# Two rotary chunks of an input projection moved ahead of the gates' chunks, in a two-layer diffusion trunk on one core

## The chip, the core and the metric

The kernel runs on one NeuronCore of a Trainium2 chip. The metric is the time of one launch on the device, in microseconds. The core has five engines with instruction queues of their own, and each works through its queue in order: PE (TensorE, matrix products), DVE (VectorE), ACT (ScalarE), POOL (GpSimd), and SP (SyncE), which issues nearly all DMAs here. A weight load of PE is shown apart, as PEld.

## The reference, cut to what matters

Two layers over 9 blocks of 128 tokens: block 0 is the prompt, blocks 1 to 8 are latent tokens on a grid. Each layer projects its input `h` once, splits the result, and feeds three mixers:

```
z = einsum('bsd,dn->bsn', h, w_in[l])
hq, hff, hfb, hi, hg, mq, mkv, mkr, gq, gk, gv = split(z, IN_OFFSETS)
hg_out = _hgrn_mixer(hq, hff, hfb, hi, hg, ...)      # gated scan, forward and backward
q_nope, q_pe = _mla_queries(mq, ...); ckv = _rms(mkv, ...)
gq = _rope_2d(_rms(gq, gqa_q_norm), row, col)        # latent tokens only
gk = _rope_2d(_rms(gk, gqa_k_norm), row, col)
mixed = concat([hg_out, mla_out, gqa_out]); y = mixed @ w_out[l]
```

The scan needs the query part `hq`, the two gates `hff`, `hfb` and the input `hi`. The rotary queries and keys `gq`, `gk` are wanted by the second attention alone. A layer norm, a SwiGLU and another layer norm end the layer. All of it is float32; most products are made of three passes on a high and a low half of the operands.

## The kernel before, in words

A layer is phase_b (input projection and forward scan), phase_c (both attentions, with the backward scan beside them), phase_d (output projection) and phase_e (SwiGLU). The change is in `phase_b`.

The projection's columns are cut into chunks of 256 (the last of 288). Chunk 0 is `hq`, written transposed. The others go through `token_chunk`: the weights are loaded and split into halves (`w_in`, `wsplit`), and for each of the 9 token blocks 24 products of 128x256 (three passes, eight slices of the depth) fill one PSUM buffer, which an evacuation function then takes away. I call one such block of a chunk a *tile*. Chunks 1 and 2 are the gates (`ev_f`: two sigmoids on ACT), 4 and 3 are `hi` and `hg` (`ev_raw`: a copy and a store), 5 and 6 are the rotary queries and keys (`ev_q`), `"b"` holds the keys and values (`ev_k`), and 7 the queries of the other attention (`ev_m`).

`ev_q` is the long one. ACT squares the tile and copies it to a stage buffer (L403, L404); DVE sums the squares (L407); POOL makes the reciprocal root in two instructions (L118, L119); DVE scales by it and by the norm's weights (L410, L412, the latter twice in chunk 6); POOL turns the pairs in `rope` (two products L392, one L395, one sum L396; not for block 0); SP stores the result to DRAM (L419). There are three stage buffers for all evacuations (`stage`, tag `st`), and a buffer is free again when its store has landed. PSUM buffers for the tiles: two in layer 0, three in layer 1 (`banks`, ring `A`).

`gates` takes logarithms, and `hgrn` is the scan: for each of the 9 token blocks a `prep` (transposes and running sums), eight levels (`levels`: DVE makes differences L636 and L639, ACT exponentials L641, POOL two products L643 and L645, PE small products L650, DVE a masked copy L655), and `out` (L674, L677, L684). I call these nine *scan blocks*. The stores of all chunks (`zq`, `zi` and so on) are read back from DRAM by later steps.

`gqa_turn` reads the stored rotary queries and keys back (L521, L525, L526), transposes them on PE (L529), and splits them on ACT and POOL (L532, L536, L537, L104); ten such turns for head group 1 are written in the loop of chunk 7, but their buffers lie where the scan's buffers (`b`) lay, so they can't start before the scan has ended. The attention's first transposed probabilities (L801) follow.

What sets the order on the engines: the instructions are handed to a scheduler that lists them per engine by a model of the time, the earlier written ones first, later written ones where an engine would wait. So chunks written behind `hgrn` are woven into its gaps on PE. In layer 0 `self.fill()` adds, at four tiles of each chunk, a step of the modulation's products (L177) from a generator.

Of the kernel before, what the change touches and what calls it, by code (L numbers as in the profile page):

```python
# [53 lines left out]
class Build:  # L54
# [275 lines left out]
    def phase_b(self, l, first=None):  # L330
# [19 lines left out]
        def token_chunk(name, evac):  # L350
            ws = self.w_in(*name)
            n = 288 if name[1] == "b" else 256
            for t in range(NT):
                ps = self.ps("A")
                terms = [(self.hts(t, k, 0), self.hts(t, k, 1), hi[:, k - k0, :], lo[:, k - k0, :])
                         for k0, k1, hi, lo in ws for k in range(k0, k1)]
                self.mm3(ps[:, :n], terms)
                evac(t, ps)
                if t % 2:
                    self.fill()  # L360

        def stage():
            return self.t("b2", [P, 384], tag="st", bufs=3)

        def ev_raw(name):
            def ev(t, ps):
                st = stage()
                nc.scalar.copy(st[:, :256], ps[:, :256])
                nc.sync.dma_start(z[name][t], st[:, :256])
            return ev  # L370

        def ev_f(d):
            def ev(t, ps):
                nc.scalar.activation(lf[:, d, t, :], ps[:, :256], AF.Sigmoid)
                self.last_sig = nc.scalar.activation(kk[:, d, t, :], ps[:, :256], AF.Sigmoid, scale=-1.0)  # L375
            return ev

        def tables(t):
            tb = self.t("b2", [P, 192], tag="tb", bufs=2)
            nc.sync.dma_start(tb, A["rope_tok"][:, t - 1, :])  # L380
            return tb

        def rope(x, tb, off, heads, half):

            w = 4 * half
            xv = x.rearrange("p (h a s f) -> p h a s f", h=heads, a=2, s=2)
            cos = tb[:, off:off + w].unsqueeze(1).broadcast_to([P, heads, w])
            sin = tb[:, off + w:off + 2 * w].rearrange("p (a s f) -> p a s f", a=2, s=2)
            t2 = self.tmp()
            tv = t2[:, :heads * w].rearrange("p (h a s f) -> p h a s f", h=heads, a=2, s=2)  # L390
            for s in range(2):
                nc.gpsimd.tensor_tensor(tv[:, :, :, s, :], xv[:, :, :, 1 - s, :],  # L392
                                        sin[:, :, s, :].unsqueeze(1).broadcast_to([P, heads, 2, half]), op=ALU.mult)
            xm = x.rearrange("p (h w) -> p h w", h=heads)
            nc.gpsimd.tensor_tensor(xm, xm, cos, op=ALU.mult)  # L395
            nc.gpsimd.tensor_tensor(x, x, t2[:, :heads * w], op=ALU.add)  # L396

        def ev_q(half):
            def ev(t, ps):
                st = stage()  # L400
                x = st[:, :256]
                sq = self.tmp()
                nc.scalar.activation(sq[:, :256], ps[:, :256], AF.Square)  # L403
                nc.scalar.copy(x, ps[:, :256])  # L404
                ss = self.t("small", [P, 4], tag="ss4", bufs=3)
                r = self.t("small", [P, 4], tag="r4", bufs=3)
                nc.vector.reduce_sum(ss, sq[:, :256].rearrange("p (h f) -> p h f", h=4), axis=AX.X)  # L407
                self.rsq(r, ss, 1 / 64, 4)
                xv = x.rearrange("p (h f) -> p h f", h=4)
                nc.vector.tensor_tensor(xv, xv, r.unsqueeze(2).broadcast_to([P, 4, 64]), op=ALU.mult)  # L410
                for h0, n, g in (((0, 4, 0),) if half == 0 else ((0, 2, 0), (2, 2, 64))):
                    nc.vector.tensor_tensor(xv[:, h0:h0 + n], xv[:, h0:h0 + n],  # L412
                                            rows[:, g:g + 64].unsqueeze(1).broadcast_to([P, n, 64]), op=ALU.mult)
                if t == 0:
                    if half:
                        nc.sync.dma_start(A["o_gk"][0, l].rearrange("s h f -> s (h f)"), x[:, 128:256])
                else:
                    rope(x, tables(t), 0, 4, 16)
                nc.sync.dma_start(z["q"][t][:, half * 256:half * 256 + 256], x)  # L419
            return ev  # L420
# [30 lines left out]
        for ci in range(3):  # L451
            for j in range(2):
# [3 lines left out]
                         for k0, k1, hi, lo in ws for k in range(k0, k1)]  # L456
# [4 lines left out]
                nc.sync.dma_start(z["h"][3 * ci:3 * ci + 3, :, j, :].rearrange("t p s -> p t s"),  # L461
                                  sg[:, :384].rearrange("p (t s) -> p t s", t=3))

        token_chunk((l, 1), ev_f(0))
        cst = {}
        for name, n in (("uinc", 2), ("ustr", 1)):
# [16 lines left out]
        self.hgrn(l, cst, masks)  # L483

        token_chunk((l, 3), ev_raw("g"))
        token_chunk((l, 5), ev_q(0))
        token_chunk((l, 6), ev_q(1))

        self.close("b")
        self.open("gB", side="right")  # L490
# [933 lines left out]
```

## Time and profile before

| | us |
|---|---|
| median of 3 runs | 3805.0 |
| the runs | 3798.03 to 3807.32 |
| the profiled execution | 3800.49 |
| its span, first to last instruction | 3798.7 |
| PE busy | 3690.6 (97%) |
| DVE, ACT, POOL busy | 2009.7, 1384.2, 1100.6 |

The profile shows one execution. Its page gives busy times and the granted clock of PE; the trace behind it gives each instruction's start and length. In a row of busy time by stretch, "x" counts instructions, and PEclk is the mean of the granted clock, 1.00 for 2.4 GHz and 0.50 for 1.2 GHz. A PE that waits inside a run of small products can still be shown as busy, so busy time is an upper bound of work.

### The profile page before, as it was taken

The page shows a single profiled execution, that of the slowest core. Times are in us where ns is not written, and L with a number is a line of the kernel's source. Part 1 is how long each engine was busy: PE and PEld are TensorE (multiplying, and loading weights), DVE is VectorE, ACT ScalarE, POOL GpSimd, SP SyncE. Part 2 cuts the span into 40 slices and gives each one's busy share as a digit, 9 for nine tenths or more (in the row PEclk, how much of TensorE's full clock was granted, in tenths as well). Part 3 has the DMA queues.
Part 4 walks back from the last instruction along what each step waited for, and adds up shares of the span by engine and source line. Part 5 has one row for each costly group of instructions (what it writes and reads, how often), then busy time and mean ns, then how long its engine had stood idle before and what let it go on. Part 6 is the DMA issues. An engine that isn't in the chain of part 4 may idle for free.

```text
span 3798.7 us, 60408 instructions
## 1 busy us (share of the span) xinstructions
PE 3690.6 (97%) x23734; PEld 3206.4 (84%) x23734; DVE 2009.7 (53%) x3906; ACT 1384.2 (36%) x3285; POOL 1100.6 (29%) x1394
## 2 busy tenths in 40 slices
PE   8999999999999999999999988999999999999997
PEld 6887877788788888888989878778887999999996
DVE  3488466556654333333366893665557533333336
ACT  3433476665331111111144334666654211111111
POOL 1168751111260000000432786511126600000054
PEclk9998999999999999999999998999999999999998
DMA  6321520001242122212331114100012311111121
GB/s 231 114 75 62 172 58 19 15 7 34 65 155 81 61 78 73 78 67 78 102 124 57 53 44 132 35 19 15 7 54 65 122 35 50 45 39 45 45 95 72
DMA packets 185967, 263.78 MB, mean 69 GB/s; under 512 B 68657, under 2 KB 114353, under 8 KB 185170
## 3 DMA queue, kind: packets, MB, share of 16 engines
q1 hardware_dynamic: 185682, 259.92, 21.6%
q8 instruction: 187, 3.06, 0.3%
q14 instruction: 98, 0.80, 0.1%
HBM read 218.47 MB, written 38.77 MB: 68 GB/s over the span
## 4 chain that ended last, share of the span: by engine, by line
PE 83%; DVE 6%; POOL 3%; ACT 3%; issue 2%; DMA 2%; SPq 0%; DVEq 0%; POOLq 0%; ACTq 0%
PE b L110 10%; PE b L112 10%; PE b L111 10%; PE d L850 7%; PE c L801 5%; PE a L110 5%; PE a L112 5%; PE a L111 5%; PE b L779 4%; PE a L779 3%; PE b L650 2%; PE c L110 2%; PE c L112 2%; PE c L111 2%; PE d L177 2%
## 5 line engine op out<-in xcount | busy, mean ns | idle before, releaser
L110 PE MATMUL b<-h,w 128*128 128x384 f32 x1848 | 625.4, 339 | 0.1
L111 PE MATMUL b<-h,w 128*128 128x384 f32 x1848 | 622.6, 337 | 2.1 <-DVE h L104 1.3
L112 PE MATMUL b<-h,w 128*128 128x384 f32 x1848 | 622.1, 337 | 0.0
L103 ACT CAST w<-raw 128x1024 fp32r<-128x1024 f32 (+2 forms) x192 | 198.5, 1036 | 808.1 <-PE b L111 153.9
L104 DVE TENSOR_TENSOR w<-raw,w 128x1024 fp32r<-128x1024 f32 (+3 forms) x188 | 239.9, 1281 | 455.4 <-ACT w L103 287.8
L1240 POOL TENSOR_TENSOR acc<-acc,lg 128x512 f32<-128x512 f32 x36 | 50.9, 1432 | 1285.2 <-DVE acc L1226 1281.1
L110 PEld LDWEIGHTS b<-h,w 128*128 128x128 f32 x1848 | 347.6, 188 | 26.4 <-issue 8.4
L111 PEld LDWEIGHTS b<-h,w 128*128 128x128 f32 x1848 | 348.0, 188 | 11.3 <-issue 4.2
L112 PEld LDWEIGHTS b<-h,w 128*128 128x128 f32 x1848 | 347.8, 188 | 7.0 <-issue 4.2
L850 PE MATMUL d<-pt,v 128*64 128x128 f32 x3456 | 288.8, 285 | 0.4 <-DVE m L851 0.4
L110 PE MATMUL a<-w,h 128*128 128x256 f32 (+1 forms) x960 | 284.8, 297 | 0.0
L111 PE MATMUL a<-w,h 128*128 128x256 f32 (+1 forms) x960 | 279.7, 291 | 0.0
L112 PE MATMUL a<-w,h 128*128 128x256 f32 (+1 forms) x960 | 278.8, 291 | 0.0
L801 PE MATMUL c<-ident,p 128*128 128x128 f32 x1728 | 271.4, 279 | 6.2 <-ACT p L785 2.4
L850 PEld LDWEIGHTS d<-pt,v 128*64 128x64 f32 x3456 | 186.4, 136 | 76.4 <-issue 61.2
L780 DVE TENSOR_REDUCE m<-b 128x1 f32<-128x384 f32 x346 | 188.2, 553 | 106.7 <-PE b L779 106.2
L801 PEld LDWEIGHTS c<-ident,p 128*128 128x128 f32 x1728 | 200.0, 141 | 46.6 <-issue 16.8
L785 ACT ACTIVATE p<-b,nm 128x384 f32<-128x384 f32 x346 | 198.5, 582 | 73.3 <-DVE nm L783 67.1
L110 PEld LDWEIGHTS a<-w,h 128*128 128x128 f32 x960 | 185.6, 193 | 24.7 <-ACT m L375 9.2
L111 PEld LDWEIGHTS a<-w,h 128*128 128x128 f32 x960 | 185.6, 193 | 6.0 <-issue 1.9
L112 PEld LDWEIGHTS a<-w,h 128*128 128x128 f32 x960 | 185.5, 193 | 5.3 <-issue 1.7
L103 ACT CAST m<-gate 128x384 fp32r<-128x384 f32 x132 | 67.7, 513 | 324.6 <-DVE gate L1197 324.6
(391 smaller groups left out, 8492.1 us busy)
## 6 DMA issues: line engine op xcount, KB each, us to landing
w<-in_w_ada_dram SPq DMA_DIRECT2D x96, 512.0 KB
raw<-in_w_ffn_in_dram SPq DMA_DIRECT2D x88, 512.0 KB
raw<-in_w_ffn_out_dram SPq DMA_DIRECT2D x44, 512.0 KB
raw<-in_w_in_a_dram SPq DMA_DIRECT2D x32, 512.0 KB
xs<-acc SPq DMA_DIRECT2D x36, 256.0 KB
u<-xs SPq DMA_DIRECT2D x36, 256.0 KB
raw<-in_w_out_dram SPq DMA_DIRECT2D x16, 512.0 KB
tx<-zq SPq DMA_DIRECT2D x72, 96.0 KB
```

The source lines that it names most:

```text
L103: self.nc.scalar.copy(hi, src)
L104: (eng or self.nc.vector).tensor_tensor(lo, src, hi.bitcast(F32), op=ALU.subtract)
L110: self.nc.tensor.matmul(out, ah, bh, start=i == 0, stop=False)
L111: self.nc.tensor.matmul(out, ah, bl, start=False, stop=False)
L112: self.nc.tensor.matmul(out, al, bh, start=False, stop=i == n - 1)
L177: self.nc.tensor.matmul(acc[r:r + 32, :], self.cs[:, 2 * (k + a):2 * (k + a) + 32], w[:, a], start=k < 4, stop=k >= 4)
L650: nc.tensor.matmul(ps[:, j * P:(j + 1) * P], X[r, j, :], Q[r, j, :], start=True, stop=True)
L779: nc.tensor.matmul(ps, a, bfn(c * 384, 384), start=k == 0, stop=k == len(ops) - 1)
L780: nc.vector.reduce_max(mx[:, c:c + 1], ps, axis=AX.X)
L785: nc.scalar.activation(pt[:, c * 384:(c + 1) * 384], tiles[c], AF.Exp, bias=nm, accum_out=sm[:, u, c:c + 1])
L801: nc.tensor.transpose(pt[:, (2 * i + u) * P:(2 * i + u + 1) * P], g["p"][u][:, kt * P:(kt + 1) * P], self.ident)
L850: nc.tensor.matmul(po[h * 64:(h + 1) * 64, :P], g["v"](k, h), turned[s // 2][:, o:o + P], start=k == 0, stop=k == 8)
```

## The change

The two calls for chunks 5 and 6 are written ahead of chunk 1, and so come second and third, behind chunk 0; before, they stood behind chunk 3 (seventh and eighth with the scan counted).

```diff
                 nc.sync.dma_start(z["h"][3 * ci:3 * ci + 3, :, j, :].rearrange("t p s -> p t s"),
                                   sg[:, :384].rearrange("p (t s) -> p t s", t=3))
 
+        token_chunk((l, 5), ev_q(0))
+        token_chunk((l, 6), ev_q(1))
         token_chunk((l, 1), ev_f(0))
         cst = {}
@@
         self.hgrn(l, cst, masks)
 
         token_chunk((l, 3), ev_raw("g"))
-        token_chunk((l, 5), ev_q(0))
-        token_chunk((l, 6), ev_q(1))
```

No instruction of the computation is added or removed. What moves is shown at two places of layer 0.

POOL, from the last half-splits of `h` on. Before, the next work of POOL is the scan's (L645, L607):

```order
L104 TENSOR_TENSOR h_72_246<-u_367,h_72_246 128x384
L104 TENSOR_TENSOR h_72_246<-u_383,h_72_246 128x384
L645 TENSOR_TENSOR Q_1637<-qT_1618,E_1632 128x256
L645 TENSOR_TENSOR Q_1654<-qT_1618,E_1649 128x256
L607 TENSOR_TENSOR m_467<-m_467,u_1606 128x2x256
```

After, `rsv`, `r` are the reciprocal root of one tile, `st` its stage buffer, `tb` the table of the rotation:

```order
L104 TENSOR_TENSOR h_72_246<-u_383,h_72_246 128x384
L118 TENSOR_SCALAR rsv_160_693<-ss_158_690 128x4
L119 TENSOR_TENSOR r_159_691<-rsv_160_693,mhalf_76 128x4
L118 TENSOR_SCALAR rsv_166_731<-ss_164_728 128x4
L119 TENSOR_TENSOR r_165_729<-rsv_166_731,mhalf_76 128x4
L392 TENSOR_TENSOR t_738<-st_724,tb_736 128x8x16 x2
L395 TENSOR_TENSOR st_724<-st_724,tb_736 128x256
L118 TENSOR_SCALAR rsv_176_781<-ss_174_778 128x4
L396 TENSOR_TENSOR st_724<-st_724,t_738 128x256
L119 TENSOR_TENSOR r_175_779<-rsv_176_781,mhalf_76 128x4
L392 TENSOR_TENSOR t_788<-st_774,tb_786 128x8x16 x2
```

All 18 tiles of the two chunks follow one another here, in this pattern, and the rotation of a tile (L392) stands directly behind the root of the same tile (L119).

PE, around the end of the scan. Before, the last `out` (`c_3288`) lies among tiles of chunk `"b"` (`a_4740`, `a_4787`) and modulation steps (`d_4602`), and twelve tiles follow it:

```order
L112 MATMUL a_4740<-w_4505,h_72_246 128x288
L177 MATMUL d_4602<-w_4783,csr_86 32x512 x2
L177 MATMUL d_4602<-w_4873,csr_86 32x512 x2
L677 MATMUL c_3288<-it_3054,at_3058 128x64
L110 MATMUL a_4787<-w_4493,h_74_250 128x288
L111 MATMUL a_4787<-w_4494,h_74_250 128x288
L112 MATMUL a_4787<-w_4493,h_74_250 128x288
L677 MATMUL c_3288<-it_3054,at_3058 128x64
L674 MATMUL c_3288<-Sf_1576,m_466 128x128
L677 MATMUL c_3288<-it_3054,at_3058 128x64 x2
L110 MATMUL a_4787<-w_4493,h_74_250 128x288
```

After, the last `out` (`c_4172`) has no tile behind it:

```order
L650 MATMUL b_4141<-Q_4138,X_4132 128x128 x2
L650 MATMUL b_4145<-Q_4138,X_4132 128x128 x2
L650 MATMUL b_4158<-Q_4155,X_4149 128x128 x2
L650 MATMUL b_4162<-Q_4155,X_4149 128x128 x2
L677 MATMUL c_4172<-it_3938,at_3942 128x64 x2
L674 MATMUL c_4172<-Sf_2460,m_466 128x128
L677 MATMUL c_4172<-it_3938,at_3942 128x64 x2
L529 MATMUL c_4970<-ident_75,tx_4967 128x128
L529 MATMUL c_4980<-ident_75,tx_4976 128x128 x4
L529 MATMUL c_5030<-ident_75,tx_5026 128x128 x4
```

The twelve tiles now stand inside the scan, and the scan's last levels and the turns (L529) follow one another alone.

## Rows read from the trace of the kernel before

**Rows 1.** The page: span, and busy time of PE over the span
```profile
span 3798.7 us, 60408 instructions
...
PE 3690.6 (97%) x23734; PEld 3206.4 (84%) x23734; DVE 2009.7 (53%) x3906; ACT 1384.2 (36%) x3285; POOL 1100.6 (29%) x1394
```
**Rows 2.** Busy by stretch; layers 0, 1: chunks, scan, tail; us, PE, PEld, DVE, ACT, POOL, PEclk
```profile
72.00:175.00 103.00, 102.34 (x770) 86.94 (x770) 32.57 (x60) 39.10 (x84) 3.92 (x4) 1.00 0.39 130
175.00:425.00 250.00, 242.24 (x1716) 202.19 (x1717) 203.41 (x487) 97.88 (x216) 189.68 (x267) 0.95 0.25 77
425.00:480.00 55.00, 49.10 (x354) 42.61 (x353) 16.48 (x31) 26.51 (x73) 36.89 (x69) 0.97 0.74 206
...
1984.00:2070.00 86.00, 84.93 (x723) 84.12 (x721) 49.93 (x60) 39.50 (x85) 14.63 (x6) 1.00 0.25 78
2070.00:2315.00 245.00, 228.18 (x1636) 201.41 (x1637) 200.00 (x481) 95.52 (x217) 190.54 (x275) 0.92 0.16 49
2315.00:2362.00 47.00, 38.87 (x299) 37.48 (x298) 13.31 (x25) 25.04 (x71) 34.52 (x63) 0.90 0.75 206
```
**Rows 3.** Lines L375, L677, L801 by source: min/median/max ns, first and last start
```profile
L375 ACT ACTIVATE m<-a x18: 377/378/380, 74.5 to 137.0; 128x256 f32<-128x256 f32 x18
L375 ACT ACTIVATE m<-a x12: 380/380/381, 1984.7 to 2029.5; 128x256 f32<-128x256 f32 x12
L677 PE MATMUL c<-it,at x72: 217/275/473, 199.6 to 424.6; 128*128 128x64 f32 x72
L677 PE MATMUL c<-it,at x72: 217/275/477, 2093.9 to 2314.6; 128*128 128x64 f32 x72
L801 PE MATMUL c<-ident,p x864: 270/272/332, 480.1 to 938.6; 128*128 128x128 f32 x173
L801 PE MATMUL c<-ident,p x804: 270/272/476, 2361.8 to 2798.0; 128*128 128x128 f32 x161
```
**Rows 4.** Busy by stretch: single scan blocks, two of each layer
```profile
202.60:229.50 26.90, 26.90 (x193) 21.80 (x193) 16.36 (x45) 10.54 (x22) 12.04 (x15) 1.00 0.28 87
...
336.90:367.90 31.00, 31.00 (x188) 24.77 (x187) 24.92 (x60) 12.22 (x26) 23.98 (x34) 0.75 0.14 41
...
2121.40:2147.10 25.70, 25.70 (x201) 22.79 (x201) 22.30 (x55) 9.78 (x25) 23.24 (x33) 1.00 0.10 30
...
2229.00:2259.10 30.10, 25.82 (x165) 22.98 (x165) 24.97 (x59) 11.38 (x24) 23.76 (x30) 0.82 0.20 63
```
**Rows 5.** The rotary tiles' lines on POOL and DVE by source, 236 to 386 us
```profile
L119 POOL TENSOR_TENSOR r<-rsv,mhalf x17: 1005/1058/1820, 240.7 to 381.5; 128x4 f32<-128x4 f32 x17
L118 POOL TENSOR_SCALAR rsv<-ss x17: 193/253/922, 240.0 to 381.2; 128x4 f32<-128x4 f32 x17
L392 POOL TENSOR_TENSOR t<-st,tb x28: 451/500/638, 249.5 to 374.2; 128x128 f32<-128x128 f32 x28
L395 POOL TENSOR_TENSOR st<-st,tb x14: 723/760/989, 250.4 to 374.8; 128x256 f32<-128x256 f32 x14
L396 POOL TENSOR_TENSOR st<-st,t x14: 721/845/1544, 252.5 to 377.2; 128x256 f32<-128x256 f32 x14
L410 DVE TENSOR_TENSOR st<-st,r x17: 406/754/978, 241.9 to 383.4; 128x256 f32<-128x256 f32 x17
L412 DVE TENSOR_TENSOR st<-st,rows x25: 277/505/846, 243.1 to 385.2; 128x128 f32<-128x128 f32 x16, 128x256 f32<-128x256 f32 x9
```
**Rows 6.** The chain of waits, one piece: a store of 128 KB to DRAM; start, us, what
```profile
412.15 1.74 DMA zs<-it
```
**Rows 7.** The turns: ACT's copies by source; POOL's splits by line, busy us, mean ns
```profile
L532 ACT COPY te<-c x20: 266/588/673, 432.5 to 509.5; 128x512 f32<-128x512 f32 x18, 128x128 f32<-128x128 f32 x2
L532 ACT COPY te<-c x20: 266/586/680, 2322.4 to 2393.5; 128x512 f32<-128x512 f32 x18, 128x128 f32<-128x128 f32 x2
...
L537 POOL TENSOR_TENSOR Q<-te,Q 64x384 fp32r<-64x384 f32 x18 | 18.7, 1040 | 13.2 <-ACT Q L536 12.6
L104 POOL TENSOR_TENSOR K<-te,K 128x128 fp32r<-128x128 f32 x20 | 9.2, 463 | 1.2
```

## The prediction

> **What bounds the kernel now.** I read the page's busy times first, then busy time by stretch for the two input projections, then the lines that open and close their parts, then the instructions that move. PE is busy for 97% of the span [rows 1], so the time can fall only by what PE waits or runs at 1.2 GHz, and it rises by each wait that the change adds. The change touches the stretch from the chunks to the first attention product (L801) of each layer; behind it the order of PE is the same as before. So I ask how much later or earlier the first L801 comes; before, it starts at 480.1 and 2361.8 us [rows 3].
>
> That stretch has three parts [rows 2]. In the chunks (72 to 175, 1984 to 2070) PE is full, DVE has a third to a half of the time, POOL almost nothing (3.9 and 14.6 us). In the scan (225 us in layer 0 and 220.7 in layer 1 from the first to the last `out` product, eight periods of 28.1 and 27.6 us, [rows 3]) PE, DVE and POOL are all at 76 to 97%, with a mean granted clock of 0.95 and 0.92. In the tail PE idles 5.9 of 55 us and 8.1 of 47. All that could be won: idle 7.8 + 5.9 + 16.8 + 8.1 = 39 us, and the stretches at 1.2 GHz, half of whose length is 14 and 24 us: 77 us, 2% of the span.
>
> **What moves, part by part.** Per layer 18 tiles of PE work go to the front with their evacuation; nothing is added or taken away.
>
> *The front.* A tile costs PE 2.8 us: 16 steps between the 1st and 17th tile of layer 1's gates take 44.8 us [rows 3]. In layer 0 seventeen steps take 62.5 us [rows 3], with 17 modulation products between them, so such a product costs 0.9 us. Before the scan, PE has 18 tiles more in each layer, in layer 0 also 16 modulation products (the generator is drawn on earlier), in layer 1 half a `hi` tile less: 50.4 + 14.4 = 64.8 us and 50.4 - 1.4 = 49 us.
>
> But the tiles' evacuation may be slower than PE. In the new order of POOL the rotation of a tile follows directly on its own root, and between the two DVE must scale the tile, while POOL, in order, waits. POOL's own time per tile, by the smallest values [rows 5], is 0.193 + 1.005 + 2 x 0.451 + 0.723 + 0.721 = 3.54 us; the wait for DVE 0.406 + about 0.5 and some 0.1 for two hand-overs (my estimate), so a cycle of 4.5 us. By the medians it is 3.92 + 1.4 = 5.3. The rows were taken beside a scan that keeps DVE and POOL above 75%; at the front DVE is at a third, so I take the smallest. With three stage buffers, ACT can take the 18th tile away only when the 15th has been stored: 13 rotated tiles x 4.5 + 2 unrotated x 1.2 + 4 for the first tile through PE, ACT and DVE + 1.7 for the store [rows 6] = 67 us from the start, and then the copy. PE has PSUM buffers for one more tile in layer 0 and two in layer 1; without waiting it would come to that point after 19 x 2.8 + 14.4 = 68 and 20 x 2.8 = 56 us. So layer 0 loses little (I take 2 us, since the modulation products come bunched), layer 1 about 11 (67 - 56). By the medians the evacuation needs 77 us, and the losses are 10 and 21.
>
> On this the Trainium skill bears, page "Perfetto Trace Analysis", section "Optimizing Scalar/DVE Operations": GpSimd and VectorE share an SBUF read port. By this rule the minima hold where DVE is quiet, and the sum stays 3823; with the medians it would be 3841. No run here shows yet which.
>
> *The scan.* Its blocks now have chunks 3, `"b"` and 7 as filler, 25 tiles instead of 31, and these press less on DVE and POOL (`ev_k` and `ev_m` have one norm and at most 32 columns to turn). Blocks 1 to 6 get some 20 tiles, about as many as before; block 7 gets 1.0 and none in layers 0 and 1, block 8 none in either. What a block costs PE apart from filler is read from one without a rotary tile: 202.6 to 229.5, with 3.4 tiles and 4 modulation products, takes 26.9 us with PE full: 26.9 - 9.5 - 3.6 = 13.8. In layer 1 a block with 3.6 tiles gives 25.7 - 10.1 = 15.6 [rows 4], with rotary work on DVE and POOL beside it; relieved of that I take 15. A tile of 288 columns is counted by its width, 3.15 us. Layer 0, blocks 1 to 6: 6 x 13.8 + 11.2 x 2.8 + 8.9 x 3.15 + 20 products x 0.9 = 160 us. Layer 1: 6 x 15 + 11 x 2.8 + 8.9 x 3.15 = 149 us.
>
> The uncovered blocks the trace doesn't show. From below they are bounded by DVE's own work in a block without rotary tiles, 16.4 us [rows 4]; from above by the slowest blocks with filler, 31.0 and 30.1 [rows 4], where PE stood at 0.75 and 0.82 of its clock. Their 3.1 tiles and 6 products and their 2.8 tiles taken off, these two leave 17 and 22 us. So I take 20 us for block 7, and 17.5 for block 8, which prepares no successor. The scan from first to last `out`: 160 + 37.5 = 198 us (225 before) and 149 + 37.5 = 187 (220.7 before).
>
> Here a rule of the Trainium skill speaks against the change: "Perfetto Trace Analysis", section "Optimization Strategy", says that where regimes are bound by different engines, interleaving them may help. The change takes interleaved work apart. By it alone, with no relief in blocks 1 to 6 (they keep 28.1 and 27.6 us), the scan would be 9 and 17 us longer, and the time 3849. The rows show why I don't follow it that far: all three engines are nearly full in the blocks that it would keep.
>
> *The tail.* Before, twelve tiles of `"b"` and 7 stand between the scan's end and L801 in layer 0 and 13.6 in layer 1's last block and tail, and the ten turns of head group 1 hide below them. Now the turns stand alone, since their buffers come free only with the scan's end. The first copy of a turn came 7.9 and 7.8 us behind the last `out` [rows 3, 7]; nine further turns cost POOL 1.04 + 0.46 = 1.5 us each [rows 7] and cannot go faster; I take 1.8 with the loads, and 2.5 us for scores, maximum and exponentials: 7.8 + 16 + 2.5 = 26 us. Bounds: 22 (1.5 each, 1 us behind them) and 32. What is queued behind these waits on PE is the whole attention. Before it was 480.1 - 424.6 = 55.5 and 2361.8 - 2314.6 = 47.2 us.
>
> **The sum.** Layer 0: 64.8 + 2 (front) - 27 (scan) - 29.5 (tail) = +10.3. Layer 1: 49 + 11 - 33.7 - 21.2 = +5.1. Together some +16 us; I add 2 for a slow start of the attention, whose first products now follow 26 us of little work (in layer 1 before, the tail's clock was already 0.90, [rows 2]). 3800.5 + 18 = 3818.5 for the profiled execution, which is 4.5 below the median of the three runs; on the median 3823.
>
> **The rivals.**
> *Faster.* The relief goes deeper: freed of rotary work, a covered block costs PE 10 us besides its tiles instead of 13.8 and 15. Twelve blocks x 4 to 5 us = 54, and the time is 3823 - 54 = 3769. It turns to a gain where the cost falls by over 1.5 us (18 over 12 blocks). For it: clock and idle time are worst in the blocks with DVE and POOL above 77%. Against it: the block from 202.6 had DVE at 61% and POOL at 45% and cost 13.8 all the same.
> *Even.* Turns at 22 us, no stall in layer 0 and 7 in layer 1, layer 1's blocks at 13.8: 18 - 8 - 6 - 7 = -3, so 3802. For it: each alone is an end of a bound that a row supports.
> *Worse.* Medians at the front (+18) and uncovered blocks that fall to 1.2 GHz as the worst ones did (four, 4 us each, +16): 3857.
> *The change does nothing.* Excluded: the orders differ as shown, on both engines.
>
> **How the numbers follow.** Forecast, slower by 5 to 30 us: 0.47. Even: 0.25. Worse: 0.15. Faster: 0.13, of which half is below 3794. The range must leave out two tenths: from 3794 (-11, the even case in, half of the faster one out) to 3858 (the worse case mostly in). About 0.3% (11 us) is what a measurement of this kernel can tell from no change. Faster by more: 0.13; within: 0.29, the even case and the forecast's lower edge; slower by more: 0.58.
>
> **What would show it.** Right: POOL at 75% or more in the first 70 us of layer 1's chunks and PE waiting there on an evacuation; the last `out` around 465 and 2341 us; some 26 us from it to L801, with PE below half; blocks 2 to 6 free of 1.2 GHz. Wrong: PE full at the front (then POOL's cycle is below 3 us), blocks without tiles above 25 us, turns that start before the scan's end, or covered blocks below 22 us, which would be the gain.

## The result, and the profile of the changed kernel

The changed kernel takes 3868.6 us (median of four, 3867.63 to 3869.89) against 3802.3 for the kernel before on the same chip: ratio 1.0172, interval 1.0159 to 1.0185. It is slower by 66 us. The forecast was slower by 18, at most 3858: the direction held, the size did not.

The page of the changed kernel, span and busy times (before: [rows 1]):

```profile
span 3865.8 us, 60513 instructions
...
PE 3710.2 (96%) x23734; PEld 3221.8 (83%) x23734; DVE 1985.4 (51%) x3906; ACT 1392.6 (36%) x3291; POOL 1088.0 (28%) x1394
```

The span is 67.1 us longer, PE's busy time 19.6. So 47.5 us are new idle time of PE. The rest is shown as busy with the same 23734 instructions: work at 1.2 GHz, or waiting inside a run of products. Where the idle time lies is read from the busy time by stretch, which answers to [rows 2]. First the 18 rotary tiles, then gates and `hi`, then the scan, then the bare turns, for layer 0 and for layer 1 (columns: us, then busy us of PE, PEld, DVE, ACT, POOL, the mean granted clock, DMA share, GB/s):

```profile
74.00:156.00 82.00, 64.14 (x469) 56.08 (x468) 25.96 (x62) 14.89 (x38) 51.91 (x90) 0.94 0.38 124
156.00:254.00 98.00, 97.25 (x764) 85.65 (x763) 34.99 (x69) 40.51 (x89) 10.57 (x15) 1.00 0.41 134
254.00:484.00 230.00, 220.96 (x1542) 181.92 (x1540) 175.32 (x439) 92.22 (x207) 135.10 (x203) 0.94 0.23 71
484.00:510.00 26.00, 13.55 (x52) 10.18 (x52) 3.75 (x11) 16.61 (x40) 19.08 (x27) 0.63 0.61 145
2022.00:2096.00 74.00, 57.44 (x445) 55.40 (x443) 25.36 (x58) 15.33 (x39) 50.57 (x84) 0.95 0.29 87
2096.00:2182.00 86.00, 84.67 (x718) 83.84 (x720) 51.34 (x69) 40.63 (x91) 24.66 (x23) 1.00 0.24 73
2182.00:2401.00 219.00, 207.42 (x1453) 180.10 (x1452) 172.92 (x428) 86.85 (x202) 136.82 (x204) 0.92 0.16 50
2401.00:2426.00 25.00, 13.60 (x52) 9.23 (x52) 3.74 (x11) 16.77 (x40) 19.05 (x27) 0.64 0.64 154
```

PE idles 17.9 and 16.6 us beside the rotary tiles, 9.0 and 11.6 in the scan, 12.5 and 11.4 beside the turns. DVE is quiet at the front (a third), POOL is at 63 and 68%: nobody is full there, and PE waits all the same.

The lines that open and close the parts, by source (answering to [rows 3]; min/median/max ns, first and last start):

```profile
L403 ACT ACTIVATE t<-a x18: 374/383/393, 74.4 to 156.9; 128x256 f32<-128x256 f32 x18
L677 PE MATMUL c<-it,at x72: 217/275/478, 279.1 to 484.1; 128*128 128x64 f32 x72
L677 PE MATMUL c<-it,at x72: 217/275/477, 2204.3 to 2401.1; 128*128 128x64 f32 x72
L801 PE MATMUL c<-ident,p x864: 269/273/477, 510.2 to 974.8; 128*128 128x128 f32 x173
L801 PE MATMUL c<-ident,p x864: 269/273/476, 2426.1 to 2890.1; 128*128 128x128 f32 x173
```

The scan's first level (L650), both layers before, then after:

```profile
L650 PE MATMUL b<-qT,X x72: 272/272/579, 174.9 to 395.7; 64*128 64x128 f32 x72
L650 PE MATMUL b<-qT,X x72: 272/272/579, 2070.0 to 2283.5; 64*128 64x128 f32 x72
L650 PE MATMUL b<-qT,X x72: 271/272/579, 254.3 to 461.4; 64*128 64x128 f32 x72
L650 PE MATMUL b<-qT,X x72: 271/272/579, 2181.7 to 2379.9; 64*128 64x128 f32 x72
```

From these the whole difference can be booked, in us against the kernel before. "Front" runs from the last evacuation of chunk 0 (L459: 71.4 and 1983.9 before, 71.6 and 2021.8 after) to the first level, "scan" on to the last `out`, "tail" on to the first L801:

| | layer 0, forecast | measured | layer 1, forecast | measured |
|---|---|---|---|---|
| front | +66.8 | +79.2 | +60 | +73.8 |
| scan | -27 | -19.9 | -33.7 | -25.2 |
| tail | -29.5 | -29.4 | -21.2 | -22.2 |
| first L801 to the next layer, or the end | +2 | +7.8 | 0 | +2.8 |

With 0.2 us at the start of layer 0 this adds up to 67.1. The tail was forecast to a microsecond. The front was missed by 26 us, the scan by 16, the stretch behind L801 by 9.

**The round of a rotary tile.** One period of POOL at the front of layer 0 (the trace in order of time; start, us, instruction, in brackets the idle time ahead of it):

```profile
99.16 0.88 POOL L392 TENSOR_TENSOR t<-st,tb 128x128 f32<-128x128 f32 x2 [1.05 <-issue]
100.12 0.74 POOL L395 TENSOR_TENSOR st<-st,tb 128x256 f32<-128x256 f32 x1
100.94 0.19 POOL L118 TENSOR_SCALAR rsv<-ss 128x4 f32<-128x4 f32 x1
101.21 0.72 POOL L396 TENSOR_TENSOR st<-st,t 128x256 f32<-128x256 f32 x1
101.89 1.01 POOL L119 TENSOR_TENSOR r<-rsv,mhalf 128x4 f32<-128x4 f32 x1
103.96 0.88 POOL L392 TENSOR_TENSOR t<-st,tb 128x128 f32<-128x128 f32 x2 [1.05 <-issue]
```

The period is 4.80 us: 3.54 of work, 1.05 of waiting while DVE scales the tile, 0.2 between instructions. Each instruction is within 3% of the smallest value of [rows 5], so taking the minima was right. And ACT, by source in the front of layer 1: what its wait for the next square (L403) ended on, in us and times:

```profile
  POOL st L396: 45.0, 13
  PE a L112: 3.3, 2
  PE d L112: 2.2, 1
  DVE ss L407: 1.6, 1
```

L396 is the last step of the rotation. Thirteen of the 18 squares wait for it, while of the 18 copies to a stage buffer (L404) only one waits for a store, for 1.3 us: in the trace the square of a tile starts some 0.04 us behind the L396 of the tile two before. This is not what the forecast had. The square's output and the rotation's half product both come from `self.tmp()`, a ring of two scratch buffers under one tag, so a square may need a buffer that the rotation still holds. a2 below tries whether that is the reason.

### The profile page after: what moved, and what is told of

Its sections match the earlier page's. It is cut to its first block, busy times and chain, and to the rows that moved or that the text cites. A ratio compares the mean times of both kernels' runs of the same rounds, so it can differ in the third digit from the quotient of the medians.

```text
span 3865.8 us, 60513 instructions
## 1 busy us (share of the span) xinstructions
PE 3710.2 (96%) x23734; PEld 3221.8 (83%) x23734; DVE 1985.4 (51%) x3906; ACT 1392.6 (36%) x3291; POOL 1088.0 (28%) x1394
## 3 DMA queue, kind: packets, MB, share of 16 engines
q1 hardware_dynamic: 185682, 259.92, 21.2%
## 5 line engine op out<-in xcount | busy, mean ns | idle before, releaser
L103 ACT CAST w<-raw 128x1024 fp32r<-128x1024 f32 (+2 forms) x192 | 198.5, 1036 | 823.2 <-PE b L111 159.0
L801 PE MATMUL c<-ident,p 128*128 128x128 f32 x1728 | 273.2, 280 | 4.3 <-ACT rb L844 1.7
L801 PEld LDWEIGHTS c<-ident,p 128*128 128x128 f32 x1728 | 201.8, 142 | 44.2 <-issue 16.4
L103 ACT CAST m<-gate 128x384 fp32r<-128x384 f32 x132 | 67.6, 512 | 323.6 <-DVE gate L1197 323.3
```

Source lines behind the costliest of these rows:

```text
L103: self.nc.scalar.copy(hi, src)
L801: nc.tensor.transpose(pt[:, (2 * i + u) * P:(2 * i + u + 1) * P], g["p"][u][:, kt * P:(kt + 1) * P], self.ident)
```

## The experiments

Each time is a median, each ratio is to the kernel before on the same chip. The runs were not all on one chip; the kernel before took 3802.3 to 3804.2 us beside them, so a difference between two of them is good to some 2 us. Edits are against the changed kernel where nothing else is said.

### What makes the front slow

**a1_rope_dve**: the rotation of `ev_q` on DVE instead of POOL.

```diff
-        def rope(x, tb, off, heads, half):
+        def rope(x, tb, off, heads, half, e=nc.gpsimd):
...
-                    rope(x, tables(t), 0, 4, 16)
+                    rope(x, tables(t), 0, 4, 16, nc.vector)
```

> The changed kernel, with the three rotation steps of the rotary tiles (both products, the cosine product and the sum) on DVE instead of POOL, in both layers. In the changed kernel the front of 18 rotary tiles takes 82.1 us in layer 0 and 72.8 in layer 1, where PE's own work is 64.8 and 49: 17.3 + 23.8 = 41 us over. Theory (POOL's round of 4.8 us a tile sets it, 3.5 of its own work and 1.05 of waiting for DVE): POOL keeps 0.19 + 1.01 = 1.2 us a tile, DVE gets 0.41 + 0.43 + 0.43 and some 1.4 more, 2.7, about PE's 2.8; the front falls to 65 to 70 and 50 to 56 us, the time by 30 to 41 us to about 3832. Rival (the lead that two scratch and three stage buffers give is the limit, or the stores behind it, whatever engine turns the pairs): the fronts stay within 5 us and the time within 10 us.

Measured: 3829.9 us, ratio 1.0063 (1.0048 to 1.0078), so 39 us less than the changed kernel. From chunk 0 to the first level it takes 166.5 and 141.7 us instead of 182.7 and 159.9; scan and tail keep their lengths within 1 us. The front's waiting is POOL's round, and in the changed kernel the stores or stage buffers are not its cause.

**a2_scratch**: a ring of its own for the rotation's half product; no instruction more or less.

```diff
-            t2 = self.tmp()
+            t2 = self.t("b2", [P, 256], tag="t2", bufs=2)
```

> The changed kernel, with two scratch buffers of their own for the rotation, so that the square of the next tile (L403) no longer shares a ring with it. In the changed kernel ACT's square of the tile after next starts 0.04 us behind the sum of a tile (L396). Theory (POOL's round is the limit and the lead only sets which tile ends the wait): one tile more of lead at the end of the front, 4.8 us a layer, the time falls by about 9 us. Rival 1 (the shared scratch is the limit): the front falls to PE's pace, the time by 30 to 40 us. Rival 2 (the three stage buffers hold ACT back just as far): no change, within 3 us.

Measured: 3842.5 us, ratio 1.0096 (1.0081 to 1.0111), 26 us less: between the theory and the first rival. POOL in layer 0, the trace in order of time:

```profile
107.14 0.25 POOL L118 TENSOR_SCALAR rsv<-ss 128x4 f32<-128x4 f32 x1
107.47 0.73 POOL L395 TENSOR_TENSOR st<-st,tb 128x256 f32<-128x256 f32 x1
108.15 0.87 POOL L392 TENSOR_TENSOR t<-st,tb 128x128 f32<-128x128 f32 x2
108.98 1.01 POOL L119 TENSOR_TENSOR r<-rsv,mhalf 128x4 f32<-128x4 f32 x1
109.96 0.73 POOL L396 TENSOR_TENSOR st<-st,t 128x256 f32<-128x256 f32 x1
110.64 0.92 POOL L395 TENSOR_TENSOR st<-st,tb 128x256 f32<-128x256 f32 x1
```

The steps of two tiles now alternate, and the idle 1.05 us are gone. The edit adds no instruction, but the scheduler lists POOL's anew once the ring lets it. So the wait for DVE, which the forecast took for a property of the order of POOL, is one of the ring: with the square one tile earlier, POOL has the other tile to work on. The price: with DVE at work beside it, single L395 take 0.92 instead of 0.73 and L118 0.25 instead of 0.19, and DVE pays more. Its scaling by line, layer 0, the changed kernel (93 to 118 us) and then a2 (94 to 114 us; us, mean ns):

```profile
L410 DVE TENSOR_TENSOR st<-st,r 128x256 f32<-128x256 f32 x6 | 2.6, 425 | 21.6 <-POOL r L119 21.6
```
```profile
L410 DVE TENSOR_TENSOR st<-st,r 128x256 f32<-128x256 f32 x4 | 3.2, 808 | 5.3 <-POOL r L119 3.6 <-ACT st L404 1.7
```

On this the Trainium skill, page "Perfetto Trace Analysis", section "Optimizing Scalar/DVE Operations", says that GpSimd and VectorE share an SBUF read port. The rounds, alone and beside the other engine, agree with it.

From chunk 0 to the first level a2 takes 169.8 and 151.0 us; the forecast for PE's own work gives 168.3 and 135.1. In layer 1 something still holds, and ACT shows what comes next: freed of the ring, its copies (L404) wait for the store of a stage buffer, 15.3 us in nine of them there and 14.2 us in six in layer 0, where the changed kernel had one wait of 1.3 us in all. So the three stage buffers, the forecast's limit and the second rival's, stand right behind the ring.

**b1_zip**: the same chunks ahead of the scan, but a rotary tile and a gate tile in turn.

```diff
...                       # token_chunk made a generator, and zipped, which takes tiles from two in turn
-        token_chunk((l, 5), ev_q(0))
-        token_chunk((l, 6), ev_q(1))
-        token_chunk((l, 1), ev_f(0))
+        zipped(((l, 5), ev_q(0)), ((l, 1), ev_f(0)))
...
-        token_chunk((l, 2), ev_f(1))
+        zipped(((l, 6), ev_q(1)), ((l, 2), ev_f(1)))
```

> The changed kernel with the same chunks ahead of the scan, but tile by tile: rotary chunk 5 in turn with gate chunk 1, and 6 with 2 (two rotary tiles first), the modulation steps behind each pair. Nothing else differs. Theory (POOL's round of 4.8 us a tile against PE's 2.8): a rotary tile now comes every 5.6 us, POOL keeps up, PE waits for nothing at the front, and the time falls by 35 to 41 us to about 3830. Rival (the eight weight buffers, now all held by two chunks, make PE wait for the next weights: a load and split are some 8 us before a pair): only 15 to 25 us are won. Rival (the front's loss is not the evacuation): no change.

Measured: 3841.8 us, ratio 1.0093 (1.0076 to 1.0109), 27 us less; the rival's 15 to 25 is nearer than the theory. Inside a pair PE is full (first row, busy by stretch); what is left lies mostly between the pairs (PE's longest waits in layer 0; us in total, times, longest):

```profile
75.00:100.00 25.00, 25.00 (x216) 25.00 (x216) 6.35 (x15) 5.70 (x18) 15.05 (x26) 1.00 0.23 69
```
```profile
PE a L110 <- ACT st L420: 7.9, 1, 7.9
PE a L110 <- ACT w L103: 6.7, 1, 6.7
```

The second wait is for the split of the next weights (L103), as the rival said. The first is for an evacuation (L420 is L404 of the other kernels) that stands in ACT's queue behind the copies of the scan's constants, and ACT waits 6.3 and 4.3 us there for their transfer; written behind chunk 1, they now lie between the two pairs. They pass through the same ring of two scratch buffers (`self.tmp()`): the next square starts when DVE has taken the last of them out (L494). So the order of the tiles removes POOL's bound, and holding two chunks' weights at once makes a new wait.

**a5_dve_scratch**: both edits of a1 and a2.

> The changed kernel with the rotation of the rotary tiles on DVE and two scratch buffers of its own: both measures at once, so that nothing but PE's own work (64.8 and 49 us by the forecast) should be left at the front. With DVE alone the front was 63.0 and 55.6 us over the kernel before, and ACT still waited 2 to 3 us per tile for DVE's last sum in the shared scratch. Theory: layer 1's front falls by some 5 us, the time to 3820 to 3827, and what is then over the kernel before, some 20 to 25 us, is the order alone (uncovered blocks, bare turns, slow start of the attention). Rival (DVE's own round of 3.4 us a tile is the limit): no change, 3828 to 3832.

Measured: 3830.1 us, ratio 1.0075 (1.0059 to 1.0092): no gain over a1. The theory held in layer 1 alone (137.3 us from chunk 0 to the first level, 4.4 less than in a1); layer 0 took 171.9, 5.4 more, though PE waited there for an evacuation for 2.7 us only (6.2 in a1). The modulation products show where it goes, by line, PE between chunk 0 and the first level of layer 0, a5 and then a1 (busy us, mean ns):

```profile
L177 PE MATMUL d<-w,csr 128*32 128x512 f32 x80 | 26.0, 604 | 0.0
```
```profile
L177 PE MATMUL d<-w,csr 128*32 128x512 f32 x80 | 16.5, 603 | 0.0
```

As many of them, each with the same length, cover 9.5 us more: PE stands inside their runs, shown as busy. That it waits there for the modulation's weights from DRAM is likely, but was not tried. In layer 1, without modulation, PE is near its own pace (137.3 against 135.1).

### How much of the change is good for anything

**a3_layer0**: the change in layer 0 alone.

```diff
-        token_chunk((l, 5), ev_q(0))
-        token_chunk((l, 6), ev_q(1))
+        if l == 0:
+            token_chunk((l, 5), ev_q(0))
+            token_chunk((l, 6), ev_q(1))
         token_chunk((l, 1), ev_f(0))
...
         token_chunk((l, 3), ev_raw("g"))
+        if l != 0:
+            token_chunk((l, 5), ev_q(0))
+            token_chunk((l, 6), ev_q(1))
```

> The change in layer 0 alone; layer 1 keeps the order of the kernel before. By the traces of both kernels layer 0 costs 30 us up to its first attention product and 9 us behind it (6 of them in the attention's first 30 transposes, while the last turns still run), layer 1 25.5 and 3. Theory (the layers add up, each loss is made and ended inside its layer): 3802 + 39 = 3841, within 3833 to 3848. Rival (what layer 0 loses is won back, or made worse, later): under 3830 or over 3855.

Measured: 3836.0 us, ratio 1.0092 (1.0077 to 1.0107). Near the theory's 3841: the layers add up, and half of the loss is made in each.

**a4_only5** and **c3_only5_scratch**: chunk 5 alone ahead (the edit against the kernel before); in c3 with the scratch ring of a2.

```diff
+        token_chunk((l, 5), ev_q(0))
         token_chunk((l, 1), ev_f(0))
...
         token_chunk((l, 3), ev_raw("g"))
-        token_chunk((l, 5), ev_q(0))
         token_chunk((l, 6), ev_q(1))
```

> Half of the change, written plainly: chunk 5 in front of chunk 1, chunk 6 behind chunk 3 as before, the scratch ring shared as in both kernels. With a scratch of its own this order took 3807.2. Theory (the shared ring costs each front tile some 1.1 us of waiting for DVE, 8 tiles less the lead of two, so 5 to 8 us a layer): 3815 to 3825. Rival (the ring binds only from the second chunk on, since PE's and ACT's lead covers the first): 3805 to 3812.

> Chunk 5 alone ahead, written as a whole in front of gate chunk 1, chunk 6 behind chunk 3 as before, and two scratch buffers of the rotation's own. POOL's round is then some 3.7 us a tile against PE's 2.8, so nine tiles lose at most 9 x 0.9 = 8 us a layer less what the buffers hold, some 2 tiles or 5 us; the wait for weights of the paired order (7.9 and 6.7 us seen) is gone. Theory (front 25 + 3 us a layer, scan covered to its last block, tail with about 5 tiles beside the turns): 3780 to 3795. Rival (the front's loss is by chunk and not by lead, 8 us or more a layer): 3800 or more.

Measured: 3819.7 us, ratio 1.0050 (1.0035 to 1.0065), as the theory of a4 said; with the ring of its own 3807.2, ratio 1.0018 (1.0010 to 1.0027), in the range of c3's rival, so c3's theory fell. The rival's reason, a larger loss at the front, does not hold, though: PE waits for evacuations at the front for 2.7 and 2.3 us (3 forecast), while 8.8 us are lost behind the first L801 of the two layers. The shared ring costs 12 us with one chunk ahead and 26 with two.

**b2_zip5**: chunk 5 alone, in turn with chunk 1; chunk 6 stays behind chunk 3. **c2_zip5_scratch**: the same with the ring of a2.

> Half of the change: chunk 5 alone goes ahead, tile by tile in turn with gate chunk 1; chunk 6 stays behind chunk 3 as in the kernel before. 36 tiles stand behind the scan's start instead of 45 (before) or 27 (changed). Theory: the front costs 9 x 2.8 = 25 us and no waiting; the scan keeps some 30 tiles to its last block, so no block is left at 1.2 GHz, and the tail has 5 tiles beside the turns instead of 13 and none; with the covered blocks 0.5 to 1 us shorter each, the time is near the kernel before, 3785 to 3805. Rival (uncovered turns and the slow start of the attention cost as much as in the changed kernel): 3815 to 3830.

> The run with chunk 5 alone ahead, in turn with gate chunk 1 (3793.2 us), with two scratch buffers of the rotation's own. Theory (in turn with gate tiles a rotary tile has 5.6 us and POOL's round is 4.8, so the ring binds nothing there): within 5 us of 3793. Rival (it binds in the scan for chunk 6): 3780 to 3785.

Measured: 3793.2 us, ratio 0.9971 (0.9959 to 0.9983), and 3794.4, ratio 0.9972 (0.9963 to 0.9981): both times as their theories said. Half of the change, with the tiles in an order that POOL can follow, is faster than the kernel before by 8 to 11 us. In b2 all nine scan blocks have filler (the last ones PE at 100% and 2.4 GHz in both layers), and the tail is 30.5 and 27.6 us. But 1.2 GHz is not gone from the scan, as the theory had it: 321.8 to 328.7 us, for one, stand at a mean of 0.51. At the front PE waits for no evacuation, and the ring is worth nothing. Written as a whole, the same chunk ahead took 3819.7 us (a4) and with a ring of its own 3807.2 (c3): the order of the tiles is worth 26 and 13 us.

**c1_before_scratch**: the kernel before with the edit of a2. **e2_before_rope_dve**: the kernel before with the edit of a1.

> The kernel before with two scratch buffers of the rotation's own, as in the run on the scratch (which took 26 us off the changed kernel, more than the 9 expected: with a scratch of its own POOL takes two tiles in turn and no longer waits 1.05 us for DVE in each). Theory (the shared ring binds only where rotary tiles come back to back; inside the scan they come every 7 to 9 us): within 6 us of the kernel before, so the order, not the ring, is what the change pays for. Rival (the ring also holds up the scan's blocks): 10 to 25 us faster than before.

> The kernel before with the rotation of the rotary tiles on DVE, the edit that took 39 us off the changed kernel. Theory (inside the scan DVE is busy for 80 to 95% of each block with rotary tiles, POOL for 75 to 94%: 1.4 us more per tile on DVE for 36 tiles, of 4 blocks a layer, goes on the path): 3810 to 3830, slower than before. Rival (POOL's hand-overs were the limit in these blocks, as at the front): 3785 to 3800, faster.

Measured: 3793.3 us, ratio 0.9977 (0.9968 to 0.9986), and 3796.8, ratio 0.9986 (0.9977 to 0.9995). c1 lies between its theory and its rival; in e2 the rival held, and the theory fell. The ring and POOL's part held up the old order as well, by 9 and 6 us. The square by source, layer 1, c1 (answering to 2114.8 to 2259.4 and 2127.5 to 2266.8 before):

```profile
L403 ACT ACTIVATE t<-a x12: 363/384/397, 2115.0 to 2206.8; 128x256 f32<-128x256 f32 x12
L403 ACT ACTIVATE t<-d x6: 367/376/388, 2127.7 to 2214.8; 128x256 f32<-128x256 f32 x6
```

The 18 rotary tiles are through 52 us earlier, so more of `"b"` and 7 falls into the scan: scan and tail together are 279.4 us (291.8 before). Not all of it stays: up to L801 the two layers gain 18.7 us, and 12.8 of these are lost again behind it. So 9 us could be had with one line and no change of order, and the order of the change costs 45 to 49 us with that ring in both (by the ratios 1.0096 and 0.9977, or by 3842.5 and 3793.3), 66 without.

### The blocks without filler

**d1_idle_tiles**: eight tiles of products per layer behind chunk 7 whose results are not read, so the kernel does 45 us more of PE's work than the reference needs.

```diff
+            return ws     # the last line of token_chunk
...
-        token_chunk((l, 7), ev_mq)
+        ws = token_chunk((l, 7), ev_mq)
+        for t in range(8):
+            ps = self.ps("A")
+            self.mm3(ps[:, :256], [(self.hts(t, k, 0), self.hts(t, k, 1), hi[:, k - k0, :], lo[:, k - k0, :])
+                                   for k0, k1, hi, lo in ws for k in range(k0, k1)])
```

> The changed kernel with eight tiles of products per layer written behind chunk 7, whose results nobody reads: 8 x 2.8 = 22.4 us of PE work a layer, 45 us in all, added where blocks 7 and 8 and the turns stand alone. There the changed kernel has PE idle for 21 us in layer 0 at a granted clock of 0.5 to 0.85, and the attention's first 465 us take 6 us longer than in the kernel before. Theory (the missing work itself costs time through the clock: uncovered blocks 16 us over the forecast, the attention's start 9 us): the added work costs less than half of its 45 us, the time is 3845 to 3885 and the blocks and the attention's first 465 us get shorter. Rival (the clock there costs nothing, since DVE, POOL and the hand-overs bound it): the added work lies in idle time and changes nothing in the blocks, or adds its 45 us: over 3890.

Measured: 3878.9 us, ratio 1.0202 (1.0188 to 1.0216). The added 45 us cost 10. Blocks 7 and 8 by stretch, layer 0 then layer 1, first of the changed kernel, then of d1:

```profile
440.10:463.70 23.60, 20.59 (x128) 16.72 (x128) 21.99 (x55) 8.79 (x19) 16.10 (x18) 0.85 0.19 63
463.70:484.50 20.80, 14.93 (x77) 12.84 (x76) 11.98 (x32) 10.34 (x13) 10.30 (x14) 0.50 0.10 32
2360.00:2382.20 22.20, 18.50 (x103) 15.94 (x102) 19.58 (x46) 7.93 (x16) 12.24 (x15) 0.65 0.02 7
2382.20:2401.50 19.30, 14.22 (x77) 12.27 (x76) 12.79 (x34) 7.78 (x11) 10.36 (x14) 0.59 0.09 28
```
```profile
440.50:465.80 25.30, 25.19 (x190) 21.95 (x189) 21.47 (x52) 8.13 (x18) 13.69 (x18) 1.00 0.05 17
465.80:488.70 22.90, 22.90 (x183) 20.52 (x183) 11.22 (x31) 7.58 (x11) 10.37 (x14) 1.00 0.21 59
2364.50:2388.20 23.70, 23.70 (x183) 20.81 (x184) 17.49 (x45) 7.86 (x17) 12.15 (x15) 1.00 0.03 8
2388.20:2412.50 24.30, 21.25 (x148) 18.16 (x148) 14.15 (x37) 8.50 (x12) 11.05 (x14) 0.93 0.32 98
```

The time is in the theory's range, but the theory's reason is not shown: in d1 the clock stands at 1.00 or 0.93, and no block is shorter. Each is 1.5 to 5 us longer and carries 62 to 106 products more for that (the x of PE; 24 are a tile, so 2.6 to 4.4 tiles). A block with little or no filler therefore takes 19 to 24 us, and one with some three tiles more 23 to 25. What the missing filler costs is not so much a slower block as PE time that nothing uses. Whether the chain of hand-overs or the half clock holds the bare block at 20 us is not separated by this run, since it changed both the load and the clock.

The stretch from the first to the last L801 did not become shorter in layer 0 either (468.7 us against 464.6); in layer 1 it lost 1.2 (462.8 against 464.0).

## Why the forecast was wrong in size

**The bound and the part to look at: right.** PE bounds, and all but 11 of the 67 us arise between the first moved tile and L801.

**The front: wrong, the step on the buffers.** That the evacuation is slower than PE, and that POOL's round sets it, was right (a1). The price of POOL's instructions was right, 3.54 us; the round was put at 4.5 us and measured 4.80: the 1.0 us for DVE and the hand-overs, of which no row showed the 0.1 for the hand-overs, became 1.05 of waiting and 0.2 between instructions. The step that failed is "With three stage buffers, ACT can take the 18th tile away only when the 15th has been stored". It named the wrong buffer. The square waits in the shared scratch ring until the tile two before is rotated, a lead of two tiles and not the three of the stage buffers, so the 18th needs 14 rotated tiles and not 13. As a2 showed, it is also this ring that lays the wait for DVE open in every round. The second part of the miss is that the round was taken as unbroken: at the change of chunk two roots (L119) stand in a row, and splits of weights lie on DVE, so that the mean round in layer 1 is 5.2 us. Fourteen rounds took 72.9 us there, where 13 x 4.5 = 58.5 were reckoned. From PE's first product of chunk 5 to the 18th square it took 85.5 and 79.6 us, not 67; PE waited 15.6 and 16.8 us for evacuations, where 2 and 11 were allowed.

In layer 0 a second term was wrong the other way. The 16 modulation products were put at 14.4 us; they are 32 instructions, and the front's 80 cover 16.5 us where 48 covered 14.5 before, so they added 2. PE's own work there was thus less than forecast, and its idle time more than the table shows: 18.6 us in the front (0.7 before).

**The scan: half right.** Blocks 1 to 6 were put at 160 and 149 us and took 158.2 and 153.2, free of 1.2 GHz in layer 0 and but for block 6 in layer 1. The terms that were too small are the uncovered blocks: 20 and 17.5 us forecast, 23.6 and 20.8, 22.2 and 19.3 measured. The forecast's bounds were 16.4 and 22; block 8 lies within them, block 7 above, and the choice fell too near the lower end. That is 10.9 of the 16 us; why such a block takes this long stays open (d1).

**The tail: right in its sum, in part by luck.** 26 us forecast for each, 26.1 and 25.0 measured. But the first copy of a turn (L532) came 3.9 and 4.1 us behind the last `out`, not 7.8, and from the tenth to L801 it took 5.8 and 6.3, not 2.5; the nine turns between, put at 16 us, took 16.4 and 14.6. The runs that keep all 18 tiles ahead (a1, a2, a3 in layer 0, a5, b1) have 25.0 to 26.4, so it is what the bare turns take.

**Behind L801: too small.** 2 us were allowed for a slow start of the attention, 10.6 were lost. In layer 0 the 30th L801 starts 25.1 us behind the first, where it was 18.9. In that stretch the granted clock is 0.77 where it was 1.00 (busy by stretch, changed kernel, then before, then a1):

```profile
510.00:535.00 25.00, 21.10 (x130) 17.09 (x129) 11.63 (x29) 22.36 (x58) 10.96 (x18) 0.77 0.42 107
```
```profile
480.00:505.00 25.00, 22.87 (x184) 17.76 (x182) 14.82 (x40) 21.43 (x67) 9.18 (x15) 1.00 0.43 113
```
```profile
494.10:519.10 25.00, 21.09 (x144) 15.04 (x143) 13.66 (x35) 23.43 (x61) 11.49 (x19) 0.94 0.42 108
```

The missing clock, 25 x 0.23 = 5.8 us, looks like the 6.2 lost, but a1 speaks against it: there the clock is 0.94, and the 30th L801 still starts 24.2 us behind the first, with 144 PE instructions in the stretch instead of 184. So the clock goes with 0.9 of the 6.2 us at most, and the cause of the rest stays open. Of the other 4.4 us no cause was looked for.

**The rivals.** "Worse" (3857) named the two places that did cost more, the front and the uncovered blocks; the measured time lies beyond it. At the front its reason was wrong: not longer instructions beside DVE, but the ring. The uncovered blocks did stand in part at 1.2 GHz, as it said, and took 10.9 us more than forecast instead of 16; that the clock is the reason is not shown. "Faster" is refuted: covered blocks kept 24 to 27 us. "Even" needed no stall in layer 0 and turns in 22 us. The rival by the Trainium skill, 3849, was passed too. Its page "Perfetto Trace Analysis", section "Optimization Strategy", says that interleaving regimes bound by different engines may help. The runs agree further than the forecast allowed: in turn with gate tiles the same rotary tiles cost 27 us less (b1), and with half of them left in the scan the kernel is 11 us faster than before (b2).

**The signs.** PE did wait for evacuations in layer 1's chunks, but POOL stood at 68% beside the rotary tiles, not 75; the last `out` came at 484.1 and 2401.1 us, not 465 and 2341; PE was busy for 52 and 54% of the tail, not below half. Of the signs of being wrong none came.

## What to carry to other kernels

Before work is moved to where it comes back to back, ask of every ring of buffers that it uses, the small scratch ones too, who else draws from it: the ring, not the engine's busy time, sets how many items can be under way, and with it whether a hand-over between two engines hides. If an evacuation takes longer than the products that feed it, mix its tiles with others that need little evacuation, and move only so many that the stretch they leave keeps its filler to the end. When a trace shows ample room on every engine and a wait all the same, try one more buffer before another order: here one line gave 26 us in the changed kernel and 9 in the one before.

## What the runs showed that was not expected

A scan block takes nearly as long without filler: with little or none it takes 19.3 to 23.6 us, in part at 1.2 GHz, and with 2.6 to 4.4 tiles more at a clock of 0.93 to 1.00 22.9 to 25.3. And a PE shown as busy can be waiting: in a5 80 modulation products cover 26.0 us, in a1 80 of the same length 16.5.
